# Both feed-forward layers' products as one level of Strassen's form in a one-core encoder layer

## The chip, the core and the metric

One core of a Trainium2 chip runs one program: one inference step of an encoder layer. The metric is the device time of one execution in microseconds, as the median of several runs; lower is better. Of the core's engines the text speaks of TensorE (PE, with its weight loads as PEld), VectorE (DVE), ScalarE (ACT), GpSimd (POOL), and the queue of SyncE (SP), which issues nearly all DMAs.

## The reference

All 1056 tokens (1024 of a prompt, 32 of a sample) pass through

```python
def swiglu(x, w_in, w_out):
    a, b = jnp.split(x @ w_in, 2, axis=-1)
    return (jax.nn.silu(a) * b) @ w_out

x = x + 0.5 * swiglu(rms_norm(x, ffn1_norm), ffn1_w_in, ffn1_w_out)
h = rms_norm(x, mix_norm)          # one projection of 3584 columns, then two kinds of attention
...
x = x + mix @ w_out
x = x + 0.5 * swiglu(rms_norm(x, ffn2_norm), ffn2_w_in, ffn2_w_out)
```

The model width is 1024, the feed-forward width 2816, all arrays are float32. In each feed-forward layer `x @ w_in` is a product of 1056 x 1024 by 1024 x 5632, and the second one of 1056 x 2816 by 2816 x 1024. The mixer between the layers has a stick-breaking attention (8 heads) and a recurrence (4 heads), for prompt and sample.

## The kernel before

Everything is kept transposed: features on the 128 partitions, tokens along the free dimension. `x` is one tile [128, 8, 1056]. Every operand of a matmul is held in two parts, `hi` (rounded to the tensor engine's float32 form) and `lo` (the rest); `split` (L136) makes them with an ACT copy and a DVE subtraction, and a product is three matmuls (`PASSES`: hi·hi, hi·lo, lo·hi).

A feed-forward layer is `ffn` (L360 on). Its outer loop takes pairs of the 22 slabs of 128 feed-forward columns. For each slab, `half_a` and `half_b` multiply the slab of w_in's first and second half with the whole x (8 row chunks, 3 passes) for three groups of tokens of 384, 384 and 288 (`GROUPS`; L197 in `project`). DVE multiplies what comes out of PSUM with the norm's factor (L380), ACT takes silu, POOL multiplies once more with the factor (L382), DVE multiplies the second half's result (L388), and `split` makes g in two parts, which stay in SBUF. After every second slab the output products (L416) of these two slabs follow for all 8 output chunks and three groups; DVE adds each, halved, to x (L419). Weights come as `wraw` slabs of 512 KB through the SP queue, one slab ahead, and are split as they land (`Slabs`, L154).

At the start `first_ffn_part` weaves the load of x, its transposes, its gain and its norm into the first products, in an order written out by hand. With the last slab pair, `prep_chunk` (L217, L218, L225, L226) makes the mixer's operands chunk by chunk as x becomes final, and x is written to DRAM. The mixer (`project_stream`, L475, the attention and recurrence streams, `mix_stream`, L1032) is merged from generators by a hand-set order. `mix_end` (L1051, L1053) adds the last heads' part group by group and makes the operands of the second layer the same way. The last slab pair of the second layer lets `store` transpose each finished group of tokens and write it out (L1205 to L1212). Where no order is written by hand, a scheduler orders each engine's instructions by a priority that follows the program and by when their inputs are ready.

Of the kernel before, what the change touches and what calls it, by code (L numbers as in the profile page):

```python
# [16 lines left out]
P = 128  # L17
D = 1024
# [26 lines left out]
def first_consts(g, pool, w):  # L45
    nc = g.nc
    g.ident = pool.tile([P, P], F32, name="ident")
    make_identity(nc, g.ident)
    g.ones = pool.tile([P, P], F32, name="ones")
    nc.vector.memset(g.ones, 1.0)  # L50
    g.eps = pool.tile([P, 1], F32, name="eps")
    nc.vector.memset(g.eps, EPS)
    g.g1 = col(g, pool, "g1", w["ffn1_norm"].rearrange("o (c p) -> p (o c)", p=P), KC)
    g.r = pool.tile([P, T], F32, name="rstd")


def more_consts(g, pool, tmp, w):
# [8 lines left out]
    # additive causal mask: NEG where s >= t (partition t, column s)  # L66
# [6 lines left out]
    # the same on 4 stacked blocks of 32 rows  # L73
# [4 lines left out]
    # level masks of the decayed products: row s in the left half of the block of column t  # L78
# [31 lines left out]
    # forget lower bound: first row of the softmax over the two rows of logits  # L110
# [25 lines left out]
def split(nc, hi, lo, src):  # L136
    """src = hi + lo exactly, both in the tensor engine's rounded float32."""
    nc.scalar.activation(hi, src, AF.Copy)
    return nc.vector.tensor_tensor(out=lo, in0=src, in1=hi, op=ALU.subtract)


class Slabs:
    """All [128, ks, 128] weight slabs in the order of use, in two parts, each loaded one ahead of its use."""
# [4 lines left out]
    def load(self, srcs, on_pool, now=True):  # L148
# [7 lines left out]
        hi = pool.tile([P, KC, P], F32R, name="whi", tag="whi", bufs=2)  # L156
        lo = pool.tile([P, KC, P], F32R, name="wlo", tag="wlo", bufs=2)
# [34 lines left out]
def project(g, ps, wt, xs, n, step=None):  # L192
    """ps[128, TG] = slab^T @ x (token group n), x and the slab in two parts."""
    nc = g.nc
    for k in range(KC):
        for i, (a, b) in enumerate(PASSES):
            nc.tensor.matmul(ps[:, 0:gw(n)], wt[a][:, k, :], xs[b][:, k, gs(n)],  # L197
                             start=(k == 0 and i == 0), stop=(k == KC - 1 and i == len(PASSES) - 1))
        if step is not None and k % 2:
            step()  # L200


def rstd_of(g, r, ms, inv_n):
    """r = (ms * inv_n + eps) ** -0.5"""
# [6 lines left out]
def prep_chunk(g, pool, x, gain, xs, n, c, acc):  # L211
# [3 lines left out]
    w = gw(n)  # L215
    xc, gc = x[:, c, gs(n)], gain[:, c:c + 1]
    nc.scalar.activation(xs[0][:, c, gs(n)], xc, AF.Copy, scale=gc)  # L217
    nc.vector.scalar_tensor_tensor(out=xs[1][:, c, gs(n)], in0=xc, scalar=gc, in1=xs[0][:, c, gs(n)],  # L218
                                   op0=ALU.mult, op1=ALU.subtract)
    if acc is None:  # L220
        acc = g.wp.tile([P, TG], F32, name="nacc", tag="xp", bufs=3)
        nc.scalar.activation(acc[:, 0:w], xc, AF.Square)
    else:
        sq = pool.tile([P, TG], F32, name="nsq", tag="s", bufs=4)
        nc.scalar.activation(sq[:, 0:w], xc, AF.Square)  # L225
        nc.gpsimd.tensor_tensor(out=acc[:, 0:w], in0=acc[:, 0:w], in1=sq[:, 0:w], op=ALU.add)  # L226
    return acc


def prep_end(g, ms, n, acc):  # L230
    """g.r = rsqrt(mean(x^2) + eps) of token group n."""
    if n == 0:
        exp_ln_tables(g)
    g.nc.tensor.matmul(ms[:, 0:gw(n)], g.ones, acc[:, 0:gw(n)], start=True, stop=True)  # L234
    rstd_of(g, g.r[:, gs(n)], ms[:, 0:gw(n)], 1.0 / D)
# [8 lines left out]
def first_ffn_part(g, x, xs, w, pool, psp, half_a, half_b):  # L244
    """x^T, the same times the gain in two parts, and g.r, all from the natural rows, amid the first products."""
    nc = g.nc
    tiles = TP // P + 1
    mh = pool.tile([P, 1], F32, name="mh", tag="mh", bufs=1)
    nc.vector.memset(mh, -0.5)
    rows = [x_rows(w, tt)[1] for tt in range(tiles)]  # L250
    cols = [slice(tt * P, tt * P + rows[tt]) for tt in range(tiles)]
    xts = []

    def load():
        tt = len(xts)
        if tt < tiles:
            xt = pool.tile([P, D], F32, name="xt", tag=("oh", "ol")[tt % 2], bufs=3)
            nc.sync.dma_start(xt[0:rows[tt]], x_rows(w, tt)[0])
            xts.append(xt)

    parts = []

    def half(tt, c0):
        cc, R = slice(c0, c0 + 4), rows[tt]
        pn = psp.tile([P, 4, P], F32, name="pn", tag="po", bufs=3)
        for c in range(4):
            nc.tensor.transpose(pn[:, c, 0:R], xts[tt][0:R, (c0 + c) * P:(c0 + c + 1) * P], g.ident[0:R, 0:R])
        xc = x[:, cc, cols[tt]]
        nc.scalar.activation(xc, pn[:, :, 0:R], AF.Copy)
        xg = pool.tile([P, 4, P], F32, name="xg", tag="xg", bufs=3)  # L270
        nc.vector.tensor_tensor(out=xg[:, :, 0:R], in0=xc, in1=g.g1[:, cc, None].broadcast_to([P, 4, R]),
                                op=ALU.mult)
        parts.append((xg[:, :, 0:R], xs[0][:, cc, cols[tt]], xs[1][:, cc, cols[tt]], c0))
        if len(parts) > 1:
            two_parts()

    def two_parts():
        xv, hi, lo, c0 = parts.pop(0)
        if c0:
            split(nc, hi, lo, xv)  # L280
        else:
            nc.gpsimd.tensor_scalar(out=hi, in0=xv, scalar1=1.0, scalar2=0.0, op0=ALU.mult, op1=ALU.add)  # L282
            nc.vector.tensor_tensor(out=lo, in0=xv, in1=hi, op=ALU.subtract)  # L283

    rs = []

    def factor(tt):
        R = rows[tt]
        sq = pool.tile([P, T], F32, name="sq", tag="gl", bufs=3)
        ss = pool.tile([P, 1], F32, name="ss", tag="ss", bufs=3)  # L290
        nc.scalar.activation(sq[0:R, 0:D], xts[tt][0:R], AF.Square, accum_out=ss[0:R])
        r = pool.tile([P, 1], F32, name="r", tag="r", bufs=4)
        nc.gpsimd.tensor_scalar(out=r[0:R], in0=ss[0:R], scalar1=1.0 / D, scalar2=EPS, op0=ALU.mult, op1=ALU.add)
        nc.gpsimd.tensor_tensor(out=r[0:R], in0=r[0:R], in1=mh[0:R], op=ALU.pow)
        rs.append(r)

    dgs = []

    def diag(*tts):
        for tt in tts:  # L300
            R = rows[tt]
            dg = pool.tile([P, P], F32, name="dg", tag="dg", bufs=3)
            nc.vector.tensor_scalar(out=dg[0:R, 0:R], in0=g.ident[0:R, 0:R], scalar1=rs[tt][0:R, 0:1],
                                    scalar2=None, op0=ALU.mult)
            dgs.append(dg)

    def spread(n):
        # g.r of token group n: r of each token on every partition
        pr = psp.tile([P, 512], F32, name="pr", tag="pb", bufs=2)
        for i in range(3):  # L310
            tt = 3 * n + i
            R = rows[tt]
            nc.tensor.matmul(pr[:, i * P:i * P + R], g.ones[0:R, :], dgs[tt][0:R, 0:R], start=True, stop=True)
        nc.vector.tensor_copy(g.r[:, gs(n)], pr[:, 0:gw(n)])

    # parts to go between the products, each group of tokens in time for its own
    todo = [lambda: half(3, 0), lambda: (half(3, 4), diag(0, 1)), lambda: (half(4, 0), diag(2)), lambda: spread(0),
            lambda: (half(4, 4), factor(3)), lambda: half(5, 0), lambda: (half(5, 4), factor(4)),
            lambda: (two_parts(), factor(5)),
            lambda: (half(6, 0), diag(3, 4)), lambda: (half(6, 4), diag(5)), lambda: (half(7, 0), factor(6)),  # L320
            lambda: spread(1),
            lambda: half(7, 4), lambda: (half(8, 0), factor(7)), lambda: half(8, 4), lambda: (two_parts(), factor(8)),
            lambda: diag(6, 7), lambda: diag(8), lambda: None, lambda: spread(2)]

    def step():
        if todo:
            todo.pop(0)()
            if len(xts) < tiles:
                load()

    load()
    g.slabs.ahead(1, False)
    load()
    load()
    g.slabs.ahead(2, False)
# [909 lines left out]
```

## Time and profile before

| | us |
|---|---|
| median of 3 runs | 2402.37 (2400.2 to 2402.84) |
| span of the profiled execution, first to last instruction | 2395.4 |
| FFN1: start to the first projection (L475) | 0 to 807.0 |
| mixer, up to `mix_end`'s first add | 807.0 to 1587.4 |
| `mix_end` | 1587.4 to 1613.5 |
| FFN2 and the output | 1613.5 to 2395.4 |

The page gives the profiled execution's span and not its time as a run; the runs' median lies 7.0 us above the span. The stages were read from the first and last instructions of the lines named. In the page's list of groups a row is: line, engine, operation, output and inputs with their shape, count, then busy time and mean duration in ns, then the idle time before and what ended it. Matmuls overlap in TensorE, so their durations add up to more than the time they take; the chain of waits shows their pace.

### The profile page before, as it was taken

What the parts mean: (1) busy time and instruction counts of PE and PEld (TensorE: products, weight loads), DVE (VectorE), ACT (ScalarE), POOL (GpSimd) and SP (SyncE); (2) the same over time, 40 slices, a digit from 0 to 9 for tenths busy, and PEclk for the clock granted to TensorE, in tenths of its full rate; (3) what the DMA queues carried; (4) which work ended last, traced back from release to release, by engine and by line L of the source; (5) the groups of instructions that cost most, each with busy time, mean ns of one, the idle gap of its engine ahead of it and who ended that gap; (6) DMA issues with size and microseconds to landing.
All of it is one profiled execution on the core that took longest, in us unless ns stands there. A gap on an engine that the chain in (4) does not pass through costs nothing. (4 is left out here: it accounts for less than half of the span.)

```text
span 2395.4 us, 34898 instructions
## 1 busy us (share of the span) xinstructions
PE 2305.0 (96%) x14394; PEld 2230.3 (93%) x14394; DVE 1262.2 (53%) x2144; ACT 812.7 (34%) x1603; POOL 474.9 (20%) x469
## 2 busy tenths in 40 slices
PE   7999999999999999998999998989999999999999
PEld 6999999999999888888888887889999999999999
DVE  6444334444433658678688688364334444333444
ACT  5111111111111656576585684244111111111111
POOL 3101111010111434243243322241110100111010
PEclk9999999999999999999999999999999999999999
DMA  4111111111111311111111112432111111111111
GB/s 126 53 45 53 50 39 45 40 50 45 53 53 36 105 46 30 33 58 38 50 42 36 56 42 92 151 113 62 43 47 36 45 45 53 53 44 45 36 45 73
DMA packets 177903, 132.23 MB, mean 55 GB/s; under 512 B 11024, under 2 KB 168976, under 8 KB 177744
## 3 DMA queue, kind: packets, MB, share of 16 engines
q1 hardware_dynamic: 174288, 125.67, 17.3%
q10 hardware_dynamic: 3456, 4.33, 0.6%
q8 instruction: 113, 1.85, 0.3%
q14 instruction: 46, 0.38, 0.0%
HBM read 108.84 MB, written 21.14 MB: 54 GB/s over the span
## 5 line engine op out<-in xcount | busy, mean ns | idle before, releaser
L382 POOL TENSOR_TENSOR s<-s,rstd 128x384 f32<-128x384 f32 x132 | 153.9, 1166 | 1293.9 <-ACT s L381 1293.9
L419 DVE SCALAR_TENSOR_TENSOR x<-po,x 128x384 f32<-128x384 f32 (+1 forms) x528 | 271.4, 523 | 169.4 <-PE po L416 169.2
L197 PE MATMUL pa<-xs_hi,whi 128*128 128x384 f32 (+1 forms) x1056 | 344.9, 327 | 6.4 <-POOL xs_hi L282 6.1
L416 PE MATMUL po<-gh,oh 128*128 128x384 f32 (+1 forms) x1056 | 345.1, 327 | 2.8 <-DVE x L419 2.5
L197 PE MATMUL pb<-xs_hi,whi 128*128 128x384 f32 (+1 forms) x1056 | 343.8, 326 | 0.0
L197 PE MATMUL pa<-xs_lo,whi 128*128 128x384 f32 (+1 forms) x1056 | 342.3, 324 | 0.7 <-DVE xs_lo L283 0.7
L416 PE MATMUL po<-gl,oh 128*128 128x384 f32 (+1 forms) x1056 | 342.1, 324 | 0.0
L197 PE MATMUL pa<-xs_hi,wlo 128*128 128x384 f32 (+1 forms) x1056 | 341.7, 324 | 0.0
L416 PE MATMUL po<-gh,ol 128*128 128x384 f32 (+1 forms) x1056 | 341.3, 323 | 0.0
L197 PE MATMUL pb<-xs_lo,whi 128*128 128x384 f32 (+1 forms) x1056 | 341.2, 323 | 0.0
L197 PE MATMUL pb<-xs_hi,wlo 128*128 128x384 f32 (+1 forms) x1056 | 340.9, 323 | 0.0
L381 ACT ACTIVATE s<-s 128x384 f32<-128x384 f32 x132 | 65.1, 493 | 631.8 <-DVE s L380 631.6
L475 PE MATMUL pp<-xs_hi,whi 128*128 128x384 f32 (+1 forms) x672 | 236.5, 352 | 0.3 <-DVE x L419 0.3
L380 DVE TENSOR_TENSOR s<-pa,rstd 128x384 f32<-128x384 f32 x132 | 69.2, 524 | 303.8 <-PE pa L197 297.4
L475 PE MATMUL pp<-xs_lo,whi 128*128 128x384 f32 (+1 forms) x672 | 222.5, 331 | 0.0
L475 PE MATMUL pp<-xs_hi,wlo 128*128 128x384 f32 (+1 forms) x672 | 221.3, 329 | 0.0
L388 DVE TENSOR_TENSOR s<-pb,s 128x384 f32<-128x384 f32 x132 | 69.2, 524 | 264.4 <-PE pb L197 260.6
L416 PEld LDWEIGHTS po<-gh,oh 128*128 128x128 f32 x1056 | 198.8, 188 | 9.7 <-DVE x L419 8.6
L197 PEld LDWEIGHTS pa<-xs_hi,whi 128*128 128x128 f32 x1056 | 199.2, 189 | 7.9 <-POOL xs_hi L282 7.1
L197 PEld LDWEIGHTS pa<-xs_lo,whi 128*128 128x128 f32 x1056 | 199.2, 189 | 1.7 <-DVE xs_lo L283 1.4
L197 PEld LDWEIGHTS pa<-xs_hi,wlo 128*128 128x128 f32 x1056 | 199.1, 189 | 0.0
L416 PEld LDWEIGHTS po<-gh,ol 128*128 128x128 f32 x1056 | 199.0, 188 | 0.0
(254 smaller groups left out, 4335.3 us busy)
## 6 DMA issues: line engine op xcount, KB each, us to landing
wraw<-in_ffn_w_in_dram SPq DMA_DIRECT2D x88, 512.0 KB, 3.8
wraw<-in_ffn_w_out_dram SPq DMA_DIRECT2D x44, 512.0 KB, 3.5
wraw<-in_w_in_dram SPq DMA_DIRECT2D x28, 512.0 KB, 3.7
xt<-in_x_prompt_dram SPq DMA_DIRECT2D x8, 512.0 KB, 6.6
out_dram<-y SPq DMA_DIRECT2D x8, 512.0 KB, 3.3
mraw<-mixd SPq DMA_DIRECT2D x6, 528.0 KB, 3.9
xd<-x SPq DMA_DIRECT2D x2, 1536.0 KB, 6.9
out_dram<-ko SPq DMA_DIRECT2D x16, 192.0 KB, 2.1
```

The lines of the kernel that those rows point to most:

```text
L197: nc.tensor.matmul(ps[:, 0:gw(n)], wt[a][:, k, :], xs[b][:, k, gs(n)], start=(k == 0 and i == 0), stop=(k == KC - 1 and i == len(PASSES) - 1))
L380: nc.vector.tensor_tensor(out=sv, in0=pa[:, 0:gw(n)], in1=r, op=ALU.mult)
L381: nc.scalar.activation(sv, sv, AF.Silu)
L382: nc.gpsimd.tensor_tensor(out=sv, in0=sv, in1=r, op=ALU.mult)
L388: nc.vector.tensor_tensor(out=sv, in0=pb[:, 0:gw(n)], in1=sv, op=ALU.mult)
L416: nc.tensor.matmul(po[:, 0:gw(n)], wot[jj][a][:, d, :], gt[jj][b][:, gs(n)], start=(i == 0), stop=(i == 3 * GJ - 1))
L419: nc.vector.scalar_tensor_tensor(out=x[:, d, gs(n)], in0=po[:, 0:gw(n)], scalar=0.5, in1=x[:, d, gs(n)], op0=ALU.mult, op1=ALU.add)
L475: nc.tensor.matmul(ps[:, 0:gw(n)], wt[a][:, k, :], xs[b][:, k, gs(n)], start=(k == 0 and i == 0), stop=(k == KC - 1 and i == len(PASSES) - 1))
```

## The change

The first products of a layer are seen as a 2x2 block product: the weights' rows are cut in two (512 each) and their two columns blocks are w_in's halves for the same slab; the tokens are cut in two blocks of 528 (512 of the prompt and 16 of the sample each, `NB`, `BW`). Seven block products stand for eight; the sums of weight blocks S1 to S4 are made on POOL, the sums of token blocks T1 to T4 once per layer in `prep`. The 528 tokens of a block are worked in two column pieces of 256 and 272 (`CW`). The second products are cut the same way: by halves of the feed-forward and of the output width, with the token blocks again. g is written to DRAM after each slab pair and read back as four quarters; the sums of w_out's blocks are made amid the first products and kept in DRAM, as is x until the second products.

```diff
+CW = (256, 272)
+BW = 528
+PRODUCTS = {1: ("A11", "B11"), 6: ("S2", "T2"), 5: ("S1", "T1"), 7: ("S3", "T3"), 2: ("A12", "B21"),
+            3: ("S4", "B22"), 4: ("A22", "T4")}
+def prep(g, xc, rr, gain, xs, c, dst=None):
...
+    for k in range(KC):
+        nc.vector.scalar_tensor_tensor(out=dst[:, k], in0=xc[:, k], scalar=gain[:, k:k + 1], in1=rr,
+                                       op0=ALU.mult, op1=ALU.mult)
+        if k == HK - 1:
+            split(nc, *xs["B11"], dst[:, 0:HK, 0, :])
...
+    split(nc, *xs["B21"], b21)
+    sub = lambda eng, out, p, q: eng.tensor_tensor(out=out, in0=p, in1=q, op=ALU.subtract)
+    sub(nc.vector, b11, b12, b11)
+    split(nc, *xs["T1"], b11)
+    split(nc, *xs["B22"], b22)
+    sub(nc.gpsimd, b12, b22, b12)
+    sub(nc.vector, b22, b22, b11)
+    split(nc, *xs["T2"], b22)
+    split(nc, *xs["T3"], b12)
+    sub(nc.vector, b21, b21, b22)
+    split(nc, *xs["T4"], b21)
+class InWeights:
...
+    def sums(self, j):
...
+        tt = nc.gpsimd.tensor_tensor
+        tt(out=s["S1"], in0=a21, in1=a22, op=ALU.add)
+        tt(out=s["S2"], in0=s["S1"], in1=a11, op=ALU.subtract)
+        tt(out=s["S3"], in0=a11, in1=a21, op=ALU.subtract)
+        tt(out=s["S4"], in0=a12, in1=s["S2"], op=ALU.subtract)
+def first_products(g, psp, pool, post, xs, wts, w_out, gd, sd, started=None, between=None):
+    order = (1, 2, 6, 5, 7, 3, 4)
+    for j in range(FC):
+        gt = post.tile([P, NB, BW], F32, name="gt", tag="gt", bufs=2)
+        for c in range(2):
...
+            tmp = lambda nm: post.tile([P, CW[1]], F32, name=nm, tag=nm, bufs=1)[:, 0:w]
+            add = lambda out, other: nc.vector.tensor_tensor(out=out, in0=ps, in1=other, op=ALU.add)
+            for i, p in enumerate(order):
+                wn, xn = PRODUCTS[p]
+                ps = psp.tile([P, 512], F32, name="bk", tag="bk", bufs=8)[:, 0:w]
+                wt = wts.get(j, wn)
+                for kk in range(HK):
+                    for n, (x, y) in enumerate(PASSES):
+                        mm = nc.tensor.matmul(ps, wt[x][:, kk, :], xs[c][xn][y][:, kk, :],
...
+                if c == 1 and i == 3:
+                    out_sums(g, pool, w_out, sd, j // 2, j % 2)
+        nc.sync.dma_start(gd[:, j], gt)
+class Second:
+    ORDER = (1, 2, 5, 3, 6, 7, 4)
...
+    def sum_t(self, p, k):
...
+        self.g.nc.gpsimd.tensor_tensor(out=q[out][:, k], in0=q[a][:, k], in1=q[b][:, k], op=ALU.subtract)
+    def split_t(self, p, k):
+        t = tile_w(self.ring, [P, BW], "t", "t", 2)
+        split(self.g.nc, *t, self.q[self.operand(p)][:, k])
+    def run(self, on=None):
+        steps = [(p, k) for p in self.ORDER for k in range(FH)]
...
+        for i, (p, k) in enumerate(steps):
+            ahead(i + 1)
...
+            for d in range(HK):
+                for c in range(2):
+                    for n, (a, b) in enumerate(PASSES):
+                        nc.tensor.matmul(banks[2 * d + c][:, 0:CW[c]], wt[a][:, d * P:(d + 1) * P], xt[b][:, cols(c)],
...
+                    if k == FH - 1:
+                        self.done(p, d, c, banks[2 * d + c][:, 0:CW[c]], s1, s5, u2)
+            for q in sums.get((p, k), ()):
+                self.sum_t(q, k)
+    def done(self, p, d, c, ps, s1, s5, u2):
...
+        elif p == 6:
+            add(nc.vector, u2[:, d, cc], ps, s1[:, d, cc])
+            add(nc.gpsimd, s5[:, d, cc], s5[:, d, cc], u2[:, d, cc])
+            add(nc.gpsimd, lo2, lo2, s5[:, d, cc])
+            add(nc.gpsimd, hi2, hi2, s5[:, d, cc])
+            add(nc.gpsimd, hi1, hi1, u2[:, d, cc])
+        elif p == 7:
+            add(nc.vector, hi2, ps, hi2)
+            add(nc.vector, hi1, ps, hi1)
-def first_ffn_part(g, x, xs, w, pool, psp, half_a, half_b):
-def ffn(g, x, xs, w_out, first=None, between=None, last=None, after=None):
```

At the start `load_tile` loads, transposes and norms the tokens of the first column piece, then `prep` makes its operands; the other piece's tiles follow, x goes to DRAM, and the second `prep` runs in place. `Second.run` accumulates one of the seven products over 11 steps in all eight PSUM banks; in each step the next step's token operand is split (`split_t`, a ring of two) and, every second step, weights. `mix_in` makes the mixer's operands during the last product and behind it; all of x is then written to DRAM. `mix_end` works in the two column pieces, writes x to DRAM, and the second layer's two `prep` calls follow it. The output's transposes follow the whole second layer. The mixer's own products and streams are as before.

More of the change, by code (lines that the diff above doesn't have):

```diff
@@ L230, in prep_end, with cols, prompt_of, block_pieces @@
[L230 to L235, printed above, removed]
+CW = (256, 272)
+BW = 528
+NB = 2
+HK = KC // 2
+FH = FC // 2
+HD = D // 2
+def cols(c):
+    return slice(0, CW[0]) if c == 0 else slice(CW[0], BW)
+def prompt_of(b, c):
+    return slice(512 * b + 256 * c, 512 * b + 256 * c + 256)
+def block_pieces(a, e):
+    edges = sorted({a, e} | {t for t in (512, TP, TP + 16) if a < t < e})
+    for p, q in zip(edges, edges[1:]):
+        if p >= TP:
+            s = p - TP
+            yield p, q, (s // 16) * BW + 512 + s % 16
+        else:
+            yield p, q, (p // 512) * BW + p % 512
@@ L241, in x_rows, with load_tile @@
     return w["x_sample"][0], TS
-def first_ffn_part(g, x, xs, w, pool, psp, half_a, half_b):
+def load_tile(g, w, pool, psp, tt, xcs, rs):
     nc = g.nc
[L247 to L280, printed above, removed]
-        else:
[L282 to L335, printed above, removed]
-    for _ in range(3):
-        load()
-    with g.tc.manual_schedule(engines=ENGINES):
-        half(0, 0)
-        half(0, 4)
-        half(1, 0)
-        g.slabs.split_next()
-        half(1, 4)
-        half(2, 0)
-        factor(0)
-        half(2, 4)
-        two_parts()
-        factor(1)
-        g.slabs.split_next()
-        factor(2)
-        wa, wb = g.slabs.get(0), g.slabs.get(0)
-        for n in range(NG):
-            last = half_b(n, wb, half_a(n, wa, step), step)
-    return last
@@ L1062, in c_free @@
-def c_free(n, d):
-    return d not in MIX_LAST
+            for b in range(NB):
+                ps = psp.tile([P, 512], F32, name="ps", tag=("z", "pp")[b], bufs=2)
+                for j, h in enumerate(MIX_LAST):
+                    for i, (p, q) in enumerate(PASSES):
+                        nc.tensor.matmul(ps[:, 0:w], lts[j][p][:, d, :], xs(q, h)[:, b * BW:(b + 1) * BW][:, cols(c)],
+                                         start=(j == 0 and i == 0), stop=(j == 1 and i == len(PASSES) - 1))
+                nc.vector.tensor_tensor(out=x[:, d, b], in0=ps[:, 0:w], in1=x[:, d, b], op=ALU.add)
@@ new lines, in mix_end @@
+            nc.sync.dma_start(xf[:, d, :, cols(c)], x[:, d])
+            if d == 0:
+                nc.scalar.activation(rr, x[:, d], AF.Square)
+            else:
+                sq = m.mo.tile([P, NB, CW[1]], F32, name="sq", tag="sq", bufs=2)[:, :, 0:w]
+                nc.scalar.activation(sq, x[:, d], AF.Square)
+                nc.gpsimd.tensor_tensor(out=rr, in0=rr, in1=sq, op=ALU.add)
+        for b in range(NB):
+            ms = psp.tile([P, 512], F32, name="ms", tag="px", bufs=3)
+            nc.tensor.matmul(ms[:, 0:w], g.ones, rr[:, b], start=True, stop=True)
+            rstd_of(g, rr[:, b], ms[:, 0:w], 1.0 / D)
@@ L1067, in tile_layer, with mix_factor @@
+def mix_factor(g, ms, a, e):
+    if a == 0:
+        exp_ln_tables(g)
+    g.nc.tensor.matmul(ms[:, 0:e - a], g.ones, g.r[:, a:e], start=True, stop=True)
+    rstd_of(g, g.r[:, a:e], ms[:, 0:e - a], 1.0 / D)
 @with_exitstack
@@ new lines, in tile_layer @@
+    for tt in (8, 2, 3, 6, 7):
+        load_tile(g, w, ldp, psp, tt, xcs, rs)
+    for c in range(2):
+        nc.sync.dma_start(xf[0][:, :, :, cols(c)], xcs[c])
+    n0s.close()
+    lds.close()
+    x1s, x1p = pool_of("f1x1")
+    xs[1] = open_operands(g, x1p, 1)
+    prep(g, xcs[1], rs[1], g.g1, xs[1], 1)
+    c1s.close()
+    a2s, a2 = pool_of("f1b", "right")
+    first_products(g, psp, a2, a2, xs, wts, w["ffn1_w_out"], gd[0], sd[0], between=consts)
+    for st in (a2s, a1s, x1s, x0s):
+        st.close()
```

637 lines of the change are left out of this document (439 added, 198 removed).

## The prediction

> **What bounds the kernel now.** I read the page first, then the busy time by stage (windows over the five stages), then the chain of waits in one of the feed-forward stages.
>
> ```profile
> span 2395.4 us, 34898 instructions
> PE 2305.0 (96%) x14394; PEld 2230.3 (93%) x14394; DVE 1262.2 (53%) x2144; ACT 812.7 (34%) x1603; POOL 474.9 (20%) x469
> ...
> 110.60:742.20 631.60, 631.60 (x3917) 630.20 (x3916) 258.84 (x434) 107.86 (x164) 65.18 (x55) 1.00 0.15 46
> ...
> 1613.50:2359.80 746.30, 746.27 (x4616) 744.14 (x4617) 305.63 (x507) 143.77 (x217) 81.52 (x71) 1.00 0.15 44
> ```
>
> The columns after a stretch are its length, then busy PE, PEld, DVE, ACT and POOL, the granted clock, DMA share and GB/s. The two feed-forward layers are pure TensorE: busy for all of their 631.60 and 746.30 us at clock 1.00, with DVE at 41%, ACT under 20% and POOL at 11%. There only the time that a matmul takes of the queue counts. Overlapping matmul durations (0.34 us) do not give it; the chain does, because it steps from one start to the next:
>
> ```profile
> 1623.48 3.19 PE pa L197 x24
> ...
> 1627.16 11.62 PE pb L197 x72
> ...
> 1964.58 11.44 PE pa L197 x71
> ...
> 2034.37 5.79 PE pa L197 x33
> ```
>
> The 24 matmuls of 288 columns take 3.19 us, 132.9 ns each. The 72 of one slab are 48 of 384 columns and 24 of 288, so one of 384 takes (11.62-3.19)/48 = 175.6 ns. One pass over two slab pairs and their output products lasts 2034.37-1964.58 = 69.79 us; a layer is 11 of them, 767.7 us.
>
> **The matmuls.** Before, a layer issues 4752 matmuls of 352 columns on average. After: 22 x 2 x 7 x 12 = 3696 in `first_products` and 77 x 24 = 1848 in `Second.run`, 5544 in all, half of 256 and half of 272 columns; that is 7/8 of the columns. The line through 288 and 384 columns (0.445 ns a column, 4.8 ns fixed) gives 118.7 and 125.8 ns. The attention has matmuls of 256 columns in the same data type, one after another:
>
> ```profile
> 1238.71 0.28 PE L703 MATMUL av<-sbl,V 128*128 128x256 f32 x1
> 1238.84 0.28 PE L703 MATMUL av<-sbh,V 128*128 128x256 f32 x1
> 1238.96 0.28 PE L703 MATMUL av<-sbl,V 128*128 128x256 f32 x1
> 1239.07 0.28 PE L703 MATMUL av<-sbh,V 128*128 128x256 f32 x1
> ```
>
> Three spacings in 0.36 us are 120 ns, so no floor of weight loads shows at this width. A layer then is 2772 x (118.7+125.8) ns = 677.8 us, 89.9 less; both layers 179.8 less. This is the whole gain; the rest is what it costs.
>
> The Trainium skill ("TensorE: Matmul & The Clock Gate", Back-to-back issue gap) gives N/2.4 + 2.5 ns, 109.2 and 115.8 ns here. By that, 288 columns would take 122.5 ns, and the trace has 132.9, so it does not agree; its result stands as rival D.
>
> **Does the rest keep up in the steady part?** Rows by line and shape:
>
> ```profile
> L419 DVE SCALAR_TENSOR_TENSOR x<-po,x 128x288 f32<-128x288 f32 x176 | 80.4, 457 | 55.2 <-PE po L416 55.2
> L139 DVE TENSOR_TENSOR wlo<-wraw,whi 128x1024 fp32r<-128x1024 f32 x88 | 108.0, 1227 | 45.1 <-ACT whi L138 45.1
> L139 DVE TENSOR_TENSOR sbl<-pt,sbh 128x512 fp32r<-128x512 f32 x48 | 32.7, 682 | 9.7 <-ACT sbh L138 9.2
> L138 ACT ACTIVATE whi<-wraw 128x1024 fp32r<-128x1024 f32 x88 | 93.3, 1060 | 181.8 <-PE pb L197 79.4 <-PE pa L197 76.7 <-DMA xd<-xp 25.7
> L620 ACT ACTIVATE t<-t 128x512 f32<-128x512 f32 x48 | 30.2, 629 | 11.8 <-DVE t L615 11.1
> L381 ACT ACTIVATE s<-s 128x288 f32<-128x288 f32 x44 | 18.9, 429 | 7.0 <-DVE s L380 7.0
> L948 POOL TENSOR_TENSOR hk<-hk,hf 128x512 f32<-128x512 f32 x28 | 43.1, 1538 | 99.9 <-PE pl L937 96.2 <-DVE hf L953 3.7
> L226 POOL TENSOR_TENSOR nacc<-nacc,nsq 128x288 f32<-128x288 f32 x14 | 12.2, 874 | 5.6 <-ACT nsq L225 5.2
> ```
>
> One slab pair of the first part is 168 matmuls, 20.5 us. Per pair DVE has 14 adds out of PSUM (457 ns at 288 columns, so 0.43 at 264), one 1024-wide and five 512-wide splits: 6.0+1.2+3.4 = 10.7 us. ACT: 6 x 0.42 + 1.06 + 5 x 0.63 = 6.7. POOL: four sums of 512, four of 256, four products of 264: 6.2+3.2+3.4 = 12.8 us. Pieces (512 KB twice for the slabs, 512 in and 512 out for the w_out sums, 540 of g) make 2.6 MB in 20.5 us, 127 GB/s:
>
> ```profile
> GB/s 126 53 45 53 50 39 45 40 50 45 53 53 36 105 46 30 33 58 38 50 42 36 56 42 92 151 113 62 43 47 36 45 45 53 53 44 45 36 45 73
> ```
>
> A slice already moved 151. So nothing exceeds PE, and 22 pairs run at 20.5 us; if POOL's cover went, a late sum S4 would first stop product 3, seven products after its inputs land. I cost it at nothing.
>
> In the second part a step is 24 matmuls, 2.93 us. It needs ACT 0.65 then DVE 0.70 for the token operand, every second step 1.06 and 1.23 for weights, and POOL about 1.55 for the next difference in 44 of the 77 steps. The ring `t` has two buffers, so the next split starts when a step starts: 1.4 us plus waits against 2.93. It fits. At the product borders it doesn't quite: product 7 has 16 DVE adds from PSUM, 6.9 us, and the next split waits behind them (with its own 1.4 us 5.4 us late); the other five have 8, 3.5 us, about 1 us late. I take 11 us a layer, **22**; bounds 10 (adds and splits interleave) and 90 (each of the 44 steps late by half a POOL instruction too, 34 us a layer).
>
> **The two starts.** Before, the projections begin at 806.97, so FFN1 took 39.3 us beside its matmuls; from mix_end's first add (L1053, 1587.4) to FFN2's first product (1613.5) pass 26.1 us.
>
> ```profile
> 8.74 3.67 PE L267 MATMUL pn<-ident,xt 128*128 128x128 f32 x16 [1.09 <-DMA xt<-in_x_prompt_dram]
> ...
> 806.97 0.41 PE L475 MATMUL pp<-xs_hi,whi 128*128 128x384 f32 x1 [0.32 <-DVE x L419]
> ...
> 1587.43 1.48 DVE L1053 TENSOR_TENSOR x<-ps,x 128x384 f32<-128x384 f32 x3
> 1589.82 0.61 DVE L218 SCALAR_TENSOR_TENSOR xs_lo<-x,g,xs_hi 128x384 fp32r<-128x384 f32 x1
> 1590.05 9.02 POOL L226 TENSOR_TENSOR nacc<-nacc,nsq 128x384 f32<-128x384 f32 x7 [25.24 <-ACT nsq L225]
> ...
> 1590.81 0.91 DVE L218 SCALAR_TENSOR_TENSOR xs_lo<-x,g,xs_hi 128x384 fp32r<-128x384 f32 x1
> ...
> 1613.53 4.45 PE pa L197 x24
> ```
>
> After, each half of the columns needs `prep` before its seven products: 8 gain-and-norm passes of 512 (0.61 at 384, so 0.67 each by the same share) and 10 splits or differences of 1024 on DVE: 5.4+12.3 = 17.7 us, the second half 18.6. Work for PE meanwhile is short: the tiles that empty PSUM lie where the second half's x is and wait for its `prep`, so eight banks let seven products and one more run, 11.5 us. FFN1: three x tiles were transposed at 12.4; the fourth waits for a buffer, some 15.5 us. Then DVE: 17.7 + five more tiles 6 + weight parts 3.5 + 18.6 ends at 61. The 0.61 us pass takes 0.91 while POOL runs (rows above); with POOL's sums and one difference I add 7: 68, less 11.5 gives 56.5. Loss **17** (bounds 5 and 35). FFN2: the first half's norm comes 16 us after mix_end begins (seven POOL adds of 512, 10.8 us, squares and two table functions round them); 16 + 17.7 + 5 of the other half's adds + 18.6 + 3.5 = 61, with POOL 67, less 11.5: 55.5 against 26.1. Loss **29** (10 to 50).
>
> **The other edges.** Between the parts g goes through DRAM: after the last matmul a DVE add 0.43, a POOL product 0.87, the write of g, which waits for it on SP, and behind it on that queue the first weights and g reads; then ACT 0.65 and DVE 0.70, for which PE waits.
>
> ```profile
> wraw<-in_ffn_w_in_dram SPq DMA_DIRECT2D x88, 512.0 KB, 3.8
> ...
> xd<-x SPq DMA_DIRECT2D x2, 1536.0 KB, 6.9
> ```
>
> With 3.8 for the read that is about 7 us, twice: **14** (bounds 4, if the reads pass the write, and 24). FFN1 to the projections: all x is written at the end, 4.3 MB or some 19 us at 1536 KB in 6.9, on the queue on which the second slab waits, and POOL splits the first slab behind the norm's adds. **8** (2 to 20). The transposes at the end stand behind the last product instead of beside it: **2** (0 to 4). The mixer's products (780 us) keep their columns: 0, +-5.
>
> Sum: 17+29+22+14+8+2 = 92 lost, 179.8 won, 87.8 less: span 2307.6. The median of the runs shown, 2402.4, is 7.0 above the profiled span of 2395.4 (launch and end lie around it); I keep that: **2315 us**.
>
> **The rivals.** A, the edges hide: by the scheduler's reordering the starts cost 8 and 12, turns 8, borders 10, the projections' edge 2: 2402.4-179.8+40 = 2263. For it: DVE was free 47% of the span; against it: the chains are serial within one engine.
>
> B, POOL and VectorE take turns. For it: 0.61 us became 0.91 beside POOL. If turns were complete, a step with a difference holds 1.55+0.70+0.62 = 2.87 of 2.93 us; product 7 with 32 POOL adds of 264 (0.85 each, 27 us) and 14.5 of DVE splits makes 41.7 against 32.3, product 2 38: 16 a layer, and the starts some 12 more: 2315+44 = 2359. Against it: the mean of 1227 ns over 88 splits of 1024 leaves no room for many waits. The Trainium skill ("SBUF — State Buffer", SBUF: two separate sides) calls the shared port an exclusive lock that DVE with two SBUF inputs and GpSimd hold for a whole instruction. The trace shows waits of 0.30 us, less than a POOL instruction's 1.29 (9.02/7).
>
> C, slower: the ring's split chain becomes the bound of the second part. It decides from 87.8/154 = 0.57 us over 2.93, a chain of 3.5 us a step; at 4.0 us, with a full POOL instruction ahead of either DVE split, it costs 154 x 1.07 = 165: 2480. Against it: 1.4 us by the rows, and weights can be split a pair ahead.
>
> D, the matmuls take 112.5 ns on average: 11088 x 9.75 ns = 108 less, 2208. That the change leaves out a product is excluded by the count.
>
> **How the numbers follow.** Forecast 56%, A 15, B 20, D 3, C 4, no change 2. Everything but the last two is faster: 94%; within 0.2% (what a measurement here can tell) 2%; slower 4%. The range leaves out C, D, half of A and some of B: 2262 to 2366.
>
> **What would show it.** In the chain of the changed kernel, 12 matmuls of a product in 1.42 and 1.51 us; PE gaps in the first 70 us, of about 25 us behind mix_end, and of about 7 us between the parts; DVE adds ahead of the first matmuls of product 4. It is wrong if PE waits within the steady steps, or if a 264-column matmul is far from 122 ns.

## The result and the profile after

| | before | after |
|---|---|---|
| median, us | 2401.3 (2392.9 to 2402.8, 4 runs) | 2549.3 (2547.3 to 2553.2, 4 runs) |
| span of the profiled execution, us | 2395.4 | 2545.0 |
| ratio after to before | | 1.063, 95% interval 1.061 to 1.065 |

The change makes the kernel 6.3% slower, where 3.6% less time was forecast. First the page of the changed kernel, its lines for the span, the engines' busy time, and PE and its clock in 40 slices:

```profile
span 2545.0 us, 40528 instructions
PE 2203.6 (87%) x16028; PEld 2118.5 (83%) x16028; DVE 1413.9 (56%) x2342; ACT 1002.6 (39%) x1981; POOL 1041.9 (41%) x1023
...
PE   4777799996897989998998988966777999986998
...
PEclk7888899998998999999999999987888999997999
```

PE is busy 101 us less than before (2203.6 against 2305.0), and the core takes 150 us more. The slices show where: PE is at 7 in the second to fifth slice and at 6 or 7 again in the 27th to 31st, that is at the start and in the early part of each layer's first products, and it dips once more at the beginning of each second part (slices 10 and 37). The busy time by windows, cut at these places (length, then busy PE, PEld, DVE, ACT, POOL with their counts, then granted clock, DMA share, GB/s):

```profile
95.00:344.80 249.80, 206.54 (x1514) 202.24 (x1513) 87.57 (x176) 52.81 (x108) 138.73 (x156) 0.90 0.48 146
344.80:591.90 247.10, 247.10 (x2018) 247.10 (x2017) 125.85 (x243) 75.91 (x143) 93.38 (x93) 1.00 0.27 81
592.40:886.00 293.60, 242.86 (x1848) 235.94 (x1848) 146.93 (x181) 104.24 (x164) 120.89 (x98) 0.92 0.40 132
617.40:643.00 25.60, 1.50 (x6) 1.15 (x5) 3.46 (x2) 2.22 (x3) 25.28 (x20) 0.56 0.83 332
1759.70:2011.90 252.20, 207.27 (x1514) 202.64 (x1513) 89.88 (x182) 53.08 (x109) 136.62 (x152) 0.90 0.46 140
2011.90:2259.00 247.10, 247.10 (x2018) 247.10 (x2016) 126.14 (x242) 76.16 (x142) 92.98 (x93) 1.00 0.26 81
2259.30:2530.00 270.70, 236.62 (x1849) 230.88 (x1850) 135.94 (x165) 88.31 (x132) 109.87 (x87) 0.95 0.38 128
```

The second row is the forecast kernel: PE busy all the time, 2018 matmuls in 247.1 us, 122.4 ns each (forecast 122.25), a slab pair (168) in 20.6 us (forecast 20.5). The first row is the same code nine pairs earlier: 1514 matmuls, which at 122.4 ns take 185.4 us, took 249.8. Counted by pairs of 168 matmuls, the first and the last of these nine take 20.6 us and the seven between them 26.3 to 34.7. That is **64 us** lost in FFN1, and 252.2 - 185.4 = **67 us** in FFN2, in the part whose other engines' work "I cost at nothing". DVE and ACT did no more in these nine pairs than in the twelve behind them; POOL did, 138.7 us against 93.4.

What POOL did there and not later is shown by the view of one tile, the sums of w_out's blocks (`osum`; duration in ns, then first and last start):

```profile
L332 POOL TENSOR_TENSOR osum<-oraw x22: 722/736/762, 86.6 to 305.5; 128x256 f32<-128x256 f32 x22
```

The program asks for one such block per slab pair (`out_sums`, at product 5 of the second column piece). All 22 of a layer were made between 86.6 and 305.5 us, one to three in each of the first nine pairs, and none later: the scheduler put them early, because nothing that they need holds them back. The second pair, with two blocks, still runs at 20.6 us; most of the slow pairs hold three. POOL's timeline over one of these pairs (start, length, instruction, and in brackets its idle time before and what ended it):

```profile
1884.31 1.00 POOL L332 TENSOR_TENSOR osum<-oraw 128x256 f32<-128x256 f32 x1 [4.39 <-DMA oraw<-in_ffn_w_out_dram]
...
1893.00 0.74 POOL L332 TENSOR_TENSOR osum<-oraw 128x256 f32<-128x256 f32 x1 [4.59 <-DMA oraw<-in_ffn_w_out_dram]
1893.70 0.77 POOL L378 TENSOR_TENSOR gt<-gt,a 128x272 f32<-128x272 f32 x1
...
1895.91 0.76 POOL L381 TENSOR_TENSOR gt<-gt,a 128x272 f32<-128x272 f32 x1
...
1902.90 1.29 POOL L301 TENSOR_TENSOR rS<-braw 128x512 f32<-128x512 f32 x1 [5.55 <-DMA braw<-in_ffn_w_in_dram]
...
1907.99 0.74 POOL L332 TENSOR_TENSOR osum<-oraw 128x256 f32<-128x256 f32 x1
...
1911.54 0.72 POOL L381 TENSOR_TENSOR gt<-gt,a 128x256 f32<-128x256 f32 x1
1916.22 0.73 POOL L332 TENSOR_TENSOR osum<-oraw 128x256 f32<-128x256 f32 x1 [3.96 <-DMA oraw<-in_ffn_w_out_dram]
```

Three rounds of sums start 8.7, 15.0 and 8.2 us apart, and the pair lasts as long as they do, some 31 us. A round is a chain, since `oraw` and `osum` have one buffer each: load (4 us), sums on POOL (3 us), write, next load. POOL works through its instructions in their order: while the next sum waits for its load, the gate products of the pair (L378, L381) stand behind it though their inputs are there. For the product at 1893.70 us, both inputs were done by 1885.6 (ACT's silu, L377, and before it DVE's add). The slab sums (L301) are late by one step more: the write of g stands on SP until the late gate product, and the load of the next slab (`braw`) is issued behind that write, at 1897.13 us. The waits of a stretch of six slow pairs (us in total, times, longest) show who pays:

```profile
DVE a L347 <- POOL gt L381: 133.8, 13, 13.7
ACT a L363 <- DVE a L347: 125.7, 12, 12.7
POOL osum L332 <- DMA oraw<-in_ffn_w_out_dram: 49.8, 12, 5.0
...
PE bk L354 <- ACT S2h L140: 30.3, 6, 5.3
POOL rS L301 <- DMA braw<-in_ffn_w_in_dram: 27.7, 6, 6.4
```

Read it from below: POOL waits for loads; DVE's add into `a` (one buffer) waits until the late gate product has read the `a` before; ACT's silu waits for that add; the split of S2 stands behind the silu on ACT; PE waits for S2 (and 9.8 us more, in six short waits, for the add into `a` itself). On SP it is the same in the queue of DMAs, where the loads of the next slab stand behind writes of sums and of g that are not made yet:

```profile
SPq L334 <- POOL osum L333: 61.9, 16, 7.1
SPq L282 <- POOL rS L304: 48.1, 7, 8.5
SPq L398 <- POOL gt L381: 33.7, 6, 6.4
```

The second loss lies eight steps into each second part: 25.6 us in which PE did 1.5 us of work (fourth row of the windows; 23.6 of them one wait for a weight split). SP's timeline says why: the weights' loads (L438) are issued behind sixteen loads of g, which take 22 us to issue, and two of x.

```profile
PE bk L495 <- ACT wh L446: 23.6, 1, 23.6
```

```profile
586.89 0.37 SPq L438 DMA_DIRECT2D oraw<-in_ffn_w_out_dram  x1
587.31 0.93 SPq L428 DMA_DIRECT2D qB<-gd  x2
593.89 0.32 SPq L398 DMA_DIRECT2D gd<-gt  x1
594.25 22.05 SPq L428 DMA_DIRECT2D qB<-gd  x16
616.41 3.88 SPq L431 DMA_DIRECT2D x<-xf  x2
620.38 24.43 SPq L438 DMA_DIRECT2D oraw<-in_ffn_w_out_dram  x3
```

The first load issued at 620.38 landed about 19 us later, where the one issued at 586.89 took 4.0: besides its late issue, it came behind transfers of g and x that were still under way.

Where the 237 us between the forecast span (2307.6) and the measured one lie, each from the rows above or the stages' first and last instructions:

| term | forecast, us | measured | over |
|---|---|---|---|
| start FFN1, beside matmuls | 56.5 | 74.4 | 18 |
| first products, slow pairs FFN1, FFN2 | 0, 0 | 64.4, 66.9 | 131 |
| second part FFN1 (225.9 pure, 11 borders, 7 turn) | 243.9 | 293.6 | 50 |
| start FFN2, from `mix_end`'s first add | 55.5 | 72.9 | 17 |
| second part FFN2 | 243.9 | 270.7 | 27 |
| mixer, projections' edge, tail | | | about -6 |

### The profile page after: what moved, and what is told of

It is laid out like the page before. It is cut to its first block, busy times and chain, and to the rows that moved or that the text cites. A ratio compares the mean times of both kernels' runs of the same rounds, so it can differ in the third digit from the quotient of the medians.

```text
span 2545.0 us, 40528 instructions
## 1 busy us (share of the span) xinstructions
PE 2203.6 (87%) x16028; PEld 2118.5 (83%) x16028; DVE 1413.9 (56%) x2342; ACT 1002.6 (39%) x1981; POOL 1041.9 (41%) x1023
## 5 line engine op out<-in xcount | busy, mean ns | idle before, releaser
L495 PE MATMUL bk<-th,wh 128*128 128x256 f32 (+1 forms) x1232 | 351.6, 291 | 59.7 <-ACT wh L446 46.3
L495 PE MATMUL bk<-tl,wh 128*128 128x256 f32 x1232 | 360.9, 294 | 21.4 <-DVE tl L141 21.2
L495 PE MATMUL bk<-th,wl 128*128 128x256 f32 x1232 | 353.8, 289 | 4.1 <-DVE wl L447 4.1
L495 PEld LDWEIGHTS bk<-th,wh 128*128 128x128 f32 x1232 | 235.4, 193 | 63.3 <-ACT wh L446 46.8
L626 PE MATMUL pp<-xs_a,wh 128*128 128x384 f32 (+1 forms) x1008 | 266.0, 346 | 0.2 <-DVE x L512 0.2
L495 PEld LDWEIGHTS bk<-tl,wh 128*128 128x128 f32 x1232 | 237.8, 193 | 30.1 <-DVE tl L141 27.7
L495 PEld LDWEIGHTS bk<-th,wl 128*128 128x128 f32 x1232 | 236.8, 192 | 4.7 <-DVE wl L447 4.7
L141 DVE TENSOR_TENSOR tl<-qB,th 128x528 fp32r<-128x528 f32 x154 | 144.0, 941 | 103.4 <-ACT th L140 102.7
L626 PEld LDWEIGHTS pp<-xs_a,wh 128*128 128x128 f32 x1008 | 173.8, 193 | 7.9 <-issue 1.8
L626 PE MATMUL pp<-xs_a,wl 128*128 128x384 f32 (+1 forms) x504 | 166.6, 330 | 0.0
L378 POOL TENSOR_TENSOR gt<-gt,a 128x256 f32<-128x256 f32 x88 | 67.1, 763 | 207.1 <-ACT a L377 207.1
L301 POOL TENSOR_TENSOR rS<-braw 128x512 f32<-128x512 f32 x44 | 57.9, 1315 | 206.7 <-DMA braw<-in_ffn_w_in_dram 205.6
L377 ACT ACTIVATE a<-a 128x256 f32<-128x256 f32 x88 | 37.4, 425 | 231.2 <-DVE a L347 230.7
```

The source lines that it names most:

```text
L301: tt(out=s["S1"], in0=a21, in1=a22, op=ALU.add)
L377: nc.scalar.activation(s["a2"], s["a2"], AF.Silu)
L378: nc.gpsimd.tensor_tensor(out=gt[:, 1, cc], in0=gt[:, 1, cc], in1=s["a2"], op=ALU.mult)
L495: nc.tensor.matmul(banks[2 * d + c][:, 0:CW[c]], wt[a][:, d * P:(d + 1) * P], xt[b][:, cols(c)], start=(k == 0 and n == 0), stop=(k == FH ...
L626: nc.tensor.matmul(ps[:, 0:gw(n)], wt[a][:, k, :], xs(b, k)[:, gs(n)], start=(k == 0 and i == 0), stop=(k == KC - 1 and i == len(PASSES) - 1))
```

## The experiments

"Paced", "held" below means: the scheduler keeps an engine's instruction behind a named one of the same engine. It adds no wait; it only fixes the order. Experiments 4, 8 and 9 were run four times, the others once; four runs of one kernel here lie 1.4 to 10.1 us apart, so a difference of that size is read from the trace's stages and not from the whole time.

**1. One block sum per pair.**

```diff
-                    out_sums(g, pool, w_out, sd, j // 2, j % 2)
+                    with g.tc.issue_after(wts.last_b.ins), g.tc.issue_after(pm.ins):
+                        out_sums(g, pool, w_out, sd, j // 2, j % 2)
```

`last_b` is the load of the slab's second half (SP), `pm` the last gate product of the first column piece (POOL).

> The w_out block sums of the first part (two loads, four POOL sums and a write for each) are held to one for each slab pair, behind the fourth gate product of POOL and the second weight load of SP; nothing else changes. Theory Q (queues): in the changed kernel all 22 of them ran in the first eight pairs, about three a pair, and the gate products, g writes and weight loads stood behind them in the in-order queues of POOL and SP. Then every slab pair takes 20.6 us from the second on, the 64 and 67 us lost in the first nine pairs of the two layers go, and the time is about 2549 - 125 = 2425 us. Rival P (POOL and VectorE hamper each other, so that a pair with POOL's sums, 12.8 us of POOL work, does not fit beside 10.7 us of DVE): all 22 pairs take over 20.6 us, some 23 to 26, and the time stays above 2520. Rival D (memory traffic of the second half's preparation is the cause): the first eight pairs stay at 27 to 33 us, the time at 2549.

Measured: 2420.0 us, 129 less. Its windows over pairs 2 to 12 and the ten behind them, and over ten pairs of FFN2:

```profile
95.40:321.80 226.40, 226.40 (x1850) 226.40 (x1849) 121.59 (x220) 72.65 (x132) 137.56 (x133) 1.00 0.43 130
321.80:527.70 205.90, 205.90 (x1682) 205.90 (x1681) 105.30 (x197) 63.04 (x116) 121.40 (x117) 1.00 0.43 131
1701.00:1907.00 206.00, 206.00 (x1683) 206.00 (x1682) 108.88 (x201) 65.69 (x121) 126.11 (x121) 1.00 0.43 129
```

PE is busy to the last digit from the second pair on, with POOL at 61% and 130 GB/s. Neither POOL's work, nor its neighbourhood to DVE, nor the DMA rate binds in the steady part; the working of "does the rest keep up" was right about throughput. What it left out is the order. POOL, with one block of sums in each pair, has them wait for nothing:

```profile
1776.51 0.75 POOL L381 TENSOR_TENSOR gt<-gt,a 128x256 f32<-128x256 f32 x1
1777.21 0.75 POOL L330 TENSOR_TENSOR osum<-oraw 128x256 f32<-128x256 f32 x1
```

Rivals P and D of the expectation fall.

**2. Which queue: POOL's or SP's.** The sums are left out, the loaded blocks written as they are:

```diff
-    tt(out=s[:, 0], in0=a21, in1=a22, op=ALU.add)
...
-    nc.sync.dma_start(sd[:, q, :, 256 * h:256 * h + 256], s)
+    nc.sync.dma_start(sd[:, q, :, 256 * h:256 * h + 256], raw.rearrange("p f e d -> p (f e) d"))
```

> The four POOL sums of each w_out block are left out: the loaded blocks go straight to the DRAM buffer, with the same bytes in and out and unpaced as in the changed kernel, so the output lacks the sums S1 to S4 of w_out. It parts POOL's queue from SP's. Theory Q in the form that POOL's in-order queue is what counts (gate products behind sums that wait for a DMA): the first pairs return to 20.6 us, 2425. Rival S (SP's queue alone: weight loads and g writes behind a chain of loads and writes): the first eight pairs stay near 28 to 33 us, 2549. Between: both carry a part.

Measured: 2459.6 us; ten pairs of each layer in windows:

```profile
95.00:325.50 230.50, 215.90 (x1681) 213.69 (x1680) 96.11 (x196) 60.78 (x119) 83.15 (x80) 0.96 0.53 163
1718.00:1945.90 227.90, 215.43 (x1677) 213.62 (x1676) 95.50 (x197) 60.11 (x119) 83.24 (x80) 0.96 0.52 160
```

At 122.4 ns a matmul the pairs should take 205.8 and 205.3 us: 24.7 and 22.6 are still lost, of 64.4 and 66.9. So with POOL's sums gone 62 to 66% of the loss goes. The rest is put down to SP's queue, where the write of a block now waits for its load:

```profile
SPq L327 <- DMA oraw<-in_ffn_w_out_dram: 55.3, 17, 4.7
```

Neither rival's time came out (2425 for POOL's queue alone, 2549 for SP's alone), so neither queue alone is the cause. The split is rough: without sums the blocks also ran ahead differently.

**3. The second part's weights on ACT's queue.**

```diff
-            self.g.nc.sync.dma_start(raw[:, 0:e - k0], self.src[self.WEIGHTS[p]][:, k0:e])
+            self.g.nc.scalar.dma_start(raw[:, 0:e - k0], self.src[self.WEIGHTS[p]][:, k0:e])
```

> The weight loads of the second part go out on ACT's queue in place of SP's; nothing else changes. In the changed kernel PE waits 23.6 us, in each of the two second parts, eight steps after the first of them, for a split of weights whose load stands on SP behind sixteen loads of q and two of x. Theory Q (order of the queue): the two waits shrink to under 5 us, the time falls by about 40 us to 2510. Rival D (the transfers themselves: 16.2 MB at 325 GB/s fill the DMA engines for these 25 to 50 us): the weight load lands hardly earlier, PE still waits 15 to 24 us, the time stays within 15 us of 2549.

Measured: 2511.8 us, 38 less. The first 31.7 us of the first layer's second part:

```profile
593.30:625.00 31.70, 31.10 (x247) 30.30 (x247) 13.75 (x16) 10.15 (x15) 4.20 (x4) 1.00 0.95 349
```

In the 25.6 us from 617.4, where the changed kernel had PE busy for 1.50 us at 332 GB/s, PE is now busy for 22.06 at 410 GB/s. The DMA engines are fuller than before and PE works all the same: what counted was the place in the queue, not the transfers. The second parts take 275.0 and 252.0 us, some 18 less each, of the 25.6 that stood there; the rest comes back as other waits.

**4. Both.**

> Both edits at once: one w_out block sum for each slab pair, and the second part's weight loads on ACT's queue. If both queue theories hold, the gains add: 2549 - 125 - 40 = 2384 us, that is at or a little under the kernel before. If pacing helps and the second waits are the DMA engines' own, 2425; if neither holds, 2549.

Measured: 2385.0 us (2380.6 to 2388.1), ratio to before 0.994, interval 0.992 to 0.996. The two account for 164 us of the 237, and turn the sign: with the order mended the change gains a little. What follows is about the rest: the starts (35 us over) and the second parts, 274.0 and 253.9 us of 225.9 pure.

**5. The mixer's input held back.** In the first layer two waits of PE end with a token split that stands on ACT behind this (waits of ACT in the second part of the kernel with both edits):

```profile
ACT nsq L1239 <- POOL rstd L1240: 13.1, 3, 12.0
...
ACT nsq L1239 <- POOL x L513: 5.0, 1, 5.0
```

The squares of the mixer's norm, meant for product 4, ran ahead to product 7 and waited for POOL, which had product 6's 32 adds to do.

```diff
-        split(self.g.nc, *t, self.q[self.operand(p)][:, k])
+        src = self.q[self.operand(p)][:, k]
+        self.last_t = self.g.nc.scalar.activation(t[0], src, AF.Copy)
+        self.g.nc.vector.tensor_tensor(out=t[1], in0=src, in1=t[0], op=ALU.subtract)
...
                 if todo:
-                    mix_in(g, xs_mix, fbp, sec.x, *todo.pop(0))
+                    with tc.issue_after(sec.last_t.ins):
+                        mix_in(g, xs_mix, fbp, sec.x, *todo.pop(0))
```

> On top of both edits before: the mixer's input steps, which are meant to run one beside each step of the first layer's product 4, are held on ACT behind the token split of their step. With both edits the first layer's second part still takes 276.6 us against 254.0 in the second layer, and two of its waits, 5.9 and 8.4 us, end with a token split that stands on ACT behind a square of the mixer (nsq) which waits for POOL. Theory Q (run ahead into an in-order queue, a third time): these waits go, the first layer's second part comes to 255 to 262 us, the time to about 2368. Rival E (POOL's 32 adds after product 6 delay the splits themselves): the waits move to another line, the part stays above 270, the time at 2385.

Measured: 2370.9 us (before on the same chip 2404.9); the first layer's second part 261.7 us, as expected. It is the same fault a third time.

**6. Token differences on VectorE.** `sum_t` on `nc.vector`.

> On top of that: the 44 differences of token operands in each second part run on VectorE in place of POOL. A token split on VectorE took 0.69 us where POOL stood still and 1.77 beside a difference on POOL. Theory L (VectorE and POOL wait for each other): the splits return to about 0.7 us, the differences take 0.7 on VectorE against 1.70 on POOL, the waits of PE for the low half of a token split (30.8 us in the two parts) fall under 12, each second part loses 8 to 12 us, and the time falls by some 20 us against the kernel with the paced mixer. Rival M (VectorE's own queue is then too long, 2.1 us of every 2.93 plus the adds at product borders): the waits stay or grow, the time is the same or up to 20 us longer.

Measured: 2365.2 us; second parts 255.8 and 247.3 us, 5.9 and 5.3 less; PE's waits for `tl` 19.6 us in place of 30.6. The groups by form, without the edit and with it:

```profile
L467 DVE TENSOR_TENSOR tl<-qB,th 128x528 fp32r<-128x528 f32 x154 | 157.8, 1028 | 63.5 <-ACT th L466 62.8
L461 POOL TENSOR_TENSOR qB<-qB,qB 128x528 f32<-128x528 f32 x88 | 148.6, 1717 | 135.2 <-DVE tl L467 82.6 <-DMA qB<-gd 50.9
```

```profile
L467 DVE TENSOR_TENSOR tl<-qB,th 128x528 fp32r<-128x528 f32 x154 | 120.4, 783 | 56.8 <-ACT th L466 56.4
L461 DVE TENSOR_TENSOR qB<-qB,qB 128x528 f32<-128x528 f32 x88 | 59.1, 703 | 10.5 <-DMA qB<-gd 9.3
```

DVE's two kinds together take 179.5 us in place of 157.8, and the second parts are shorter by 11.2 us in all; the whole time fell by 5.7, less than single runs can tell. Theory L holds in its direction; the sizes (8 to 12 us a part, waits under 12) were too large, so contention was only a part of the border loss.

**7. The starts.** On top of experiment 5: pair 0's slab sums and `prep`'s POOL difference on VectorE, and the write of the second half's tokens in eight pieces.

```diff
-    sub(nc.gpsimd, b12, b22, b12)
+    sub(nc.vector, b12, b22, b12)
...
-        wts.sums(0)
+        wts.sums(0, nc.vector)
...
+    for d in range(KC):
+        nc.sync.dma_start(xf[0][:, d, :, cols(1)], xcs[1][:, d])
```

> On top of the paced mixer (not of the differences on VectorE): in the two starts the slab sums of pair 0 and one token difference for each half run on VectorE in place of POOL, and the write of the second half's tokens to DRAM in the first layer is cut into eight, so that the norm, which writes the same tiles in place, waits for an eighth of it. Theory L and the write: in the first layer VectorE stood still 7.2 us for that write, which shrinks to 2 or less; in the second, eight VectorE instructions took 2.3 to 3.6 us beside POOL in place of 1.28, which gives 8 to 9 us back and costs 4. First start 6 to 9 us shorter (second pair at 86 to 89 us in place of 95.2), second start 4 to 7, the time some 12 us under the kernel with the paced mixer. Rival: the starts are bound elsewhere (x tiles that wait for buffers, splits on ACT), and under 4 us are gained.

Measured: 2361.9 us, 9 less than experiment 5. Second start 66.3 us in place of 72.1: as expected. First start 71.7 in place of 74.3, 2.6 us where 6 to 9 were expected: the wait for the write did shrink, from 7.16 us (changed kernel, first row) to 1.42 (this one, second), but DVE's four extra sums let the first matmul start at 58.4 in place of 53.9.

```profile
63.17 4.26 DVE L253 SCALAR_TENSOR_TENSOR xc<-xc,g,r 128x544 f32<-128x544 f32 x6 [7.16 <-DMA xf<-xc]
```

```profile
60.85 4.75 DVE L253 SCALAR_TENSOR_TENSOR xc<-xc,g,r 128x544 f32<-128x544 f32 x6 [1.42 <-DMA xf<-xc]
```

**8. All edits.**

> All edits so far together: paced sums, weights on ACT's queue, paced mixer input, token differences on VectorE, and the two starts. If they are independent, their gains add: 2371 - 6 (differences) - 9 (starts) = 2356 us, 0.98 of the kernel before. If the differences on VectorE and the starts hamper each other, 2360 to 2366.

Measured: 2347.2 us (2346.4 to 2347.7), ratio 0.978, interval 0.977 to 0.980. By ratios to the before of each chip the parts gave 0.980, so they add.

**9. A third buffer in the token ring.**

```diff
-        t = tile_w(self.ring, [P, BW], "t", "t", 2)
+        t = tile_w(self.ring, [P, BW], "t", "t", 3)
...
-            ahead(i + 1)
+            ahead(i + 2)
```

> As the one with all edits, with three buffers in place of two in the ring of token splits, and each split made two steps ahead in place of one. It asks what holds the second parts at 256 and 247 us, where 77 steps of 2.93 are 226. Theory R (depth: at a product's border the adds out of PSUM, 3.5 to 6.9 us of VectorE, stand before the next split, and one step of 2.93 us ahead does not cover them): a second step ahead covers the borders of eight adds, the waits for tl fall from 20 us to under 8, and each second part comes to 232 to 240 us, the time to about 2335. Rival W (weights: splits of w_out with two buffers, or PSUM's banks, stop PE at the border): the waits move there, the parts stay within 4 us, the time at 2356.

Measured: 2336.5 us (2330.9 to 2341.0), ratio 0.973, interval 0.971 to 0.975. PE's waits in the second parts:

```profile
PE bk L499 <- ACT th L466: 11.9, 3, 5.7
...
PE bk L499 <- DVE tl L467: 6.9, 6, 1.8
```

The waits for `tl` fall from 16.2 us (19.6 in experiment 6) to 6.9, as theory R has it, and the parts from 253.4 and 246.5 to 245.2 and 240.4 us. That is 8 and 6 us, more than rival W allows and short of the 232 to 240 of theory R: depth was a part of the border loss. The edit also makes every second step's weight split one step earlier, so it does not part tokens from weights. This kernel has the change's seven products throughout; it is 2.7% faster than the kernel before, 21 us above the forecast.

## Why the prediction was wrong

**The matmuls: right.** 122.4 ns measured against 122.25; no floor of weight loads at 256 columns, and rival D's 112.5 ns falls. The gain of 179.8 us is there: the kernel of experiment 1 runs its steady pairs at the forecast pace throughout.

**The step that failed: "Does the rest keep up in the steady part? ... I cost it at nothing."** The sums of engines' busy time and of bytes were right (experiment 1 shows PE at 100% with them), but they say only that the work fits if each pair has its own share. `out_sums` uses inputs of the program alone and its result is needed only in the second part, hundreds of us later, so nothing held it to its pair; the scheduler put up to three into each of the first pairs, and each brings a DMA wait into POOL's queue and a POOL wait into SP's. The prediction named product 3 and sum S4 as the place that would stop first; PE stopped at product 6, for S2, the third in the order. "PE waits within the steady steps" was the prediction's own sign of being wrong. Cost: 131 us, shown by experiment 1 (129 off); without it the changed kernel would have been within 1% of the kernel before.

**The turns, 7 us each: the wait named did not come, another one did.** At the turn itself PE goes on after 0.5 us (last matmul of the first part 591.9, first of the second 592.4), and after 0.3 in the second layer. The prediction had the first weights and g reads behind the write of g; in the trace a weight load and two g reads stand 6.6 us and more ahead of that write (586.89 and 587.31 against 593.89). That is its own lower bound, "if the reads pass the write". What it did not price are the reads behind the first: the next weight loads stood behind 22 us of issues, which cost 25.6 us, eight steps on. Experiment 3 gave back 38 us in both layers.

**The borders, 11 us a layer: too small.** With the order mended (experiment 5) the second parts still have 36 and 27 us over the pure 225.9. Two buffers and one step ahead did not cover the borders (experiment 9: 8 and 6 us), and DVE and POOL wait for each other (experiment 6: 6 and 5). What keeps the last 19 and 15 us stays open; PE's largest waits left there are those for `th`, ACT's half of the token split (11.9 us).

**The starts, 56.5 and 55.5: 74.4 and 72.9.** FFN1: the second `prep` ended at 83.3 us in place of 68. Of this, 7.2 us are the write of x, which `prep` overwrites in place: a wait that the sum left out. The rest was there before it: the first `prep` ran from 24.5 to 48.6 us, where the sum has 15.5 to 33.2; why stays open. FFN2: the sum of DVE work was close (its last split ends 70.3 us behind `mix_end`'s first add, forecast 67), but PE had done only two of the "seven products and one more" before it stopped, and then waited 35.9 us, since the slab's split S2 stood behind all of `prep`: about 9 of the 11.5 us taken off were not there. This is read from the traces; only the 9 us of experiment 7 are shown.

**The rivals.** A, the edges hide, falls: the starts cost 18 and 17 us more than forecast. B had a mechanism of the second parts and of the second start, but moving the work off POOL gave back only some 11 and 6 us, not the sign. C, the only slower one, put the bound in the ring; its chain cost what experiments 6 and 9 gave back, 25 us of its 165. The way in which it did go, work that runs ahead into in-order queues, was no rival of mine, and the 4% for slower hung on a mechanism that was not the one. Two of the rivals' sums are slightly off (B's 16 us a layer add up to 15, D's 2208 to 2207); nothing hangs on either.

## What to carry over

Throughput per step is half of the check; the other half is, for each engine and DMA queue, which instruction may be moved ahead to where, and what then stands behind its wait. Work whose inputs are ready from the start and whose result is needed late is the first suspect: fix its place in the order. When a kernel loses time in a stage whose rows all show slack, compare the early and the late steps of that stage before looking for a slower instruction.

## What the runs showed of the hardware

DVE and POOL take turns more fully than the row of 0.91 us in the prediction let me see. In the second layer's start of the changed kernel, DVE's subtractions of 1088 elements step at 2.27 us while POOL makes slab sums, and take 1.28 us right behind them:

```profile
1727.10 2.35 DVE L260 TENSOR_TENSOR x<-x 128x1088 f32<-128x1088 f32 x1
1729.37 2.35 DVE L141 TENSOR_TENSOR T31l<-x,T31h 128x1088 fp32r<-128x1088 f32 x1
...
1733.91 1.28 DVE L141 TENSOR_TENSOR T21l<-x,T21h 128x1088 fp32r<-128x1088 f32 x1
```

```profile
1728.26 2.31 POOL L303 TENSOR_TENSOR rS<-wraw,braw 128x512 f32<-128x512 f32 x1
1730.54 2.31 POOL L304 TENSOR_TENSOR rS<-wraw,rS 128x512 f32<-128x512 f32 x1
```

POOL's sums, 1.29 us each in the rows of the slow pair above, step at 2.28 here: each engine moves at the pace of both. The two durations alone add up to 2.57, so the turns are nearly full. The Trainium skill ("SBUF — State Buffer", SBUF: two separate sides) says that the port pair which DVE and POOL share is an exclusive lock for a whole instruction, with no split of its bandwidth; these rows agree with it far better than the 0.30 us on which rival B was marked down.

The granted clock fell with PE's waits: 0.56 in the stretch of 25.6 us above, 0.90 over the slow pairs, 1.00 in the pairs without waits, 0.936 over the whole span against 0.990 before (0.961 in the last kernel). So a wait of PE costs more than its own length. In FFN1's row of slow pairs 64.4 us are lost, and PE stood still for only 43.3 (249.80 less 206.54). The other 21 lie in the matmuls: they kept PE busy for 206.5 us in place of 185.4, a ratio of 0.90, which is the clock of that row.
